# Six attention value columns and two mLSTM value columns computed by seven-product units, with a gate column moved to cover them

## The chip, the core and the metric

The kernel runs on one core of a Trainium2 chip. The metric is device time in microseconds, the median of several executions. The engines named here are TensorE (PE: matrix products and transposes), VectorE (DVE), ScalarE (ACT), GpSimd (POOL) and SyncE (SP, which here issues most of the DMA transfers).

## The reference

One step of a streaming encoder layer in fp32, for 512 prompt tokens and 64 tokens of a running stream, 576 tokens of width 1024 in all:

```
h = LN1(alpha*x + 0.5*FFN1(x))                       # SwiGLU, width 2816
z = h @ w_in      # 72 columns of 128: mLSTM q, k, v, o | gates i, f | attention q, k, v | branch gates g_m, g_a
h = LN2(alpha*h + w_out(sig(g_m)*P_m(mLSTM(h)) + sig(g_a)*P_a(BandAttn(h))))
y = LN3(alpha*h + 0.5*FFN2(h))
```

The attention has 16 heads of 64, banded over 8 chunks of 64, with a relative bias and, for the running stream, 256 cached keys and values. The mLSTM has 4 heads of 256; its output is normed within each head before its gate. The outputs are y, the mLSTM's states and the attention's k and v rows.

## The kernel before

**Columns and tokens.** Activations lie with the features on the 128 partitions and the 576 tokens along the free axis. A *column* is 128 outputs of a weight matrix. Columns of `w_in` are numbered: 0 to 7 are the mLSTM's q, 8 to 15 its k, 16 to 23 its v, 24 to 31 its o, 32 to 39 the attention's q, 40 to 47 its k, 48 to 55 its v, 56 to 63 the gates g_m, 64 to 71 the gates g_a; "if" holds the i and f gates.

**Products.** Each fp32 operand is split in a high and a low part (fp32r), and a product is three matmuls, high by high, high by low, low by high (`mm`, L133; transposes have L143). ACT makes a weight's high part (wh). The low part (wl) comes from DVE (a subtraction), or, for the columns in `ADDED`, from ACT and an accumulating DMA that POOL issues (`add_lo`). `gemm` computes columns directly: 8 blocks of k, 3 matmuls each, in two token halves (256 and 320), which is 48 matmuls a column. `Units` and its subclass `Columns` compute a pair of columns by a seven-product scheme like Strassen's: 7 products x 4 blocks x 3 matmuls of 288 tokens are 84 matmuls a pair. This needs sums of the activations (`Combos`) and sums of the pair's weights (`prep`, with parts "a", "s", "t", "u", "b"), which DVE makes and ACT and DVE split. A unit's two weight tiles are loaded by SP into wu.

**Order.** PE's instructions run in the order in which the program writes them. A planned PE time (`od.now`) advances with each matmul, and `later(dt, fn)` places a step that much later in it, so that the step's instructions stand between the matmuls then due; `drain` runs all steps that are left, whatever their due time. The other engines and DMA queues are ordered by the scheduler from that program, with priorities (`hot`, `high_priority`) and explicit "issue after" constraints. Each engine and each queue works through its own order. Weights of direct columns are loaded two ahead in the sequence `plan`, by `pump`.

**Stages around the change.**

1. The first norm (`Norm` with index 0) ends FFN1. Per token half it accumulates sums (`moments`: residual, ACT square sq, two DVE additions), places `stats` on PE `L_STATS` = 1440 ns later (sums over the features as 128x1 products with onec, rows with ones_d), then `centre`, then `spread` `L_SPREAD` = 4920 ns later, then eight `apply`s. The wave of columns 48, 40, 32 and if (`WAVE_M`, from 395.57 us) runs as the halves come free: four passes over the first token half, then the second half.
2. The mLSTM's v columns 16 and 17 follow directly (427 to 440 us); their weights are prepared early (`EARLY1`, tiles eh and el). `combos.make` makes the activation sums in the meantime.
3. Nine units (440 to about 540 us) compute the other v columns, the o columns and four gate columns; `KEEP` says what is done with each result: gates and o through a sigmoid, all stored in DRAM (VD, OD, GD) and loaded back later.
4. Eight attention heads' pairs (`att_qkv(j)` and `att_core(j)`, about 540 to 790 us). For j > 0, `att_qkv` computes directly the columns 48+j (v), 40+j (k), 32+j (q); v is turned (`v_tr`) and split into vc, k is copied and split into kh (POOL) and kl (`dup`: DVE and a cast). `att_core` computes scores, softmax, its products ptl and the values. I call each j a head below.
5. Gates, then the attention's projection, then four mLSTM heads (`ml_kq`, `ml_early`, `ml_late`; to about 1047 us). In `ml_late`, `hidden(b)` gives five result blocks, `norm` (planned at 31000 ns) norms them on DVE with a reciprocal square root on POOL (mrs), and `back(e)`, 7200 and 10600 ns behind norm, transposes them back on PE. Between the heads come no columns, and after the last one the gate columns 59 to 62:

```
    FILL = ((), (), (), (59, 60, 61, 62))
    ...
        for c in FILL[h]:
            gate(c - 56, *((sgp, "sg") if c < 60 else (None, "s")))
    del st
    od.space = 0
    od.drain()
```

6. Column 63, the mLSTM's projection with the gates, w_out, LN2 and FFN2 (1165 to 1557 us).

Of the kernel before, what the change touches and what calls it, by code (L numbers as in the profile page):

```python
# [17 lines left out]
P = 128  # L18
# [68 lines left out]
def tile_layer(ctx: ExitStack, tc: tile.TileContext, ins, outs):  # L87
# [75 lines left out]
    def blank(out, like, behind=None):  # L163
# [13 lines left out]

    ADDED = {("in", c + j) for c in (32, 40, 48) for j in range(2, KT)} | {("in", c) for c in (*range(8), *range(10, 32), *range(56, 72))} \
# [67 lines left out]
    def pump(limit=2):  # L246
        while True:
# [24 lines left out]
            if c < wst["stop"] and plan[c][0][0][:2] != "ds" and c < wst["taken"] + limit and wst["used"] < NWB:  # L272
# [3 lines left out]
                if plan[c][0] == "if":  # L276

                    r3 = raw[:, :n].rearrange("p (k c) -> p k c", c=64)
                    h3 = hi.rearrange("p (k c) -> p k c", c=P)
                    act(h3[:, :, 0:64], r3)  # L280
                    tt(h3[:, :, 64:128], r3, f(h3[:, :, 0:64]), ALU.subtract)
                    parts[c] = (hi, None)
                else:
                    lo = wpool.tile([P, 1024], F32R, tag="wl", name=nm("wl"), bufs=NWB)
                    step = n if plan[c][0] not in PIECES else 512
                    for a in range(0, n, step):

                        with tc.issue_after(k0a[0].ins) if plan[c][0] == ("in", 50) else nullcontext():
# [239 lines left out]
    class Norm:  # L528
# [98 lines left out]
        def moments(self, j, hf, dh):  # L627
# [11 lines left out]
            if j == KT - 1:  # L639
                later(L_STATS, lambda: self.stats(hf))  # L640

# [7 lines left out]
        def stats(self, hf):  # L649
# [119 lines left out]
    class Combos:  # L769
# [11 lines left out]
        def put(self, n, i, ka, kb, room, behind=None):  # L781
            t, hi, lo = self.sums[2 * i + n], room(), room()
            act(hi, t)
            if n and i < 3:
                add_lo(lo, hi, t)
            else:
                with tc.issue_after(behind.ins) if behind is not None else nullcontext():
                    tt(lo, t, f(hi), ALU.subtract)
            a, b = slice(0, HT_), slice(HT_, T)
# [100 lines left out]
    class Units:  # L890
# [3 lines left out]
        def __init__(self, srcs, j0, pool, wp, combos):  # L894
            self.srcs, self.pool, self.wp, self.x = srcs, pool, wp, combos
            self.raw, self.ws, self.p = {}, {}, {}
            self.end = len(srcs)
            self.js = list(range(j0, self.end))
# [18 lines left out]
        @hot(30)  # L917
        def lead(self, j):

            hi, lo = (wpool.tile([P, 1024], F32R, tag=t, name=nm(t), bufs=NWB) for t in ("wh", "wl"))  # L920
# [56 lines left out]
        def run(self, tail):  # L977
            cur = ahead = None
            for j in self.js + [None]:
# [13 lines left out]
                if j == self.js[0]:  # L993
                    with tc.issue_after(self.lo.ins):
                        after = self.prep(j, "u")
# [311 lines left out]
    def gate_rows():  # L1307
        yield stt(t1, fx, -1.0, fx, ALU.mult, ALU.max)
        yield act(t1, t1, AF.Exp, scale=-1.0)
# [60 lines left out]
    def att_qkv(j):  # L1370
# [15 lines left out]
        if j == 0:  # L1386
            st["G"], vp, kp = G0, vp0, kp0
            with tc.issue_after(combos.added.ins):
                for e in range(2):
# [8 lines left out]
        def v_past():  # L1398
            assert valued[0] >= 3 * (j - 1)
            for b in range(2):  # L1400
                with tc.issue_after(added["in", 50].ins) if j < 2 else nullcontext():
                    pround(vc[:, 5 + b, :, 0:64], vp4[:, b])
                tt(vc[:, 5 + b, :, 64:128], vp4[:, b], f(vc[:, 5 + b, :, 0:64]), ALU.subtract, POOL)


        later(11500 if j < 2 else 6200, v_past)
        vf = vf0 if j == 0 else slot(F32)

        def v_tr():
            assert valued[0] >= 3 * (j - 1)  # L1410
            for b0, nb in ((0, 4), (4, 1)):
# [190 lines left out]

    GD = {c: away("gd") for c in (0, 1, 2, 6, 7)}
    VD, OD = [away("vd") for _ in range(KT)], [away("od") for _ in range(KT)]
# [5 lines left out]
    def keep_o(c, tiles):  # L1610
        for e in range(2):
            act(tiles[e], tiles[e], AF.Sigmoid)
            SP.dma_start(OD[c + e], tiles[e])

    def keep_g(c, tiles):
# [3 lines left out]

    KEEP = {16: keep_v, 24: keep_o, 56: keep_g, 64: keep_g}  # L1620
    pairs = [(c, b) for c in range(0, KT, 2) for b in (16, 24)][1:] + [(0, 56), (6, 64)]
    un = Columns([(b + c, b + c + 1) for c, b in pairs],
# [19 lines left out]
    with tc.tile_pool(name="cx", bufs=1, side="right", reuse_waits="tile") as cx:  # L1642
# [3 lines left out]

        def middle():
            with tc.issue_after(q0[1].ins):
                return un.prep(0, "a")
# [29 lines left out]
    for vc in vcs:  # L1679
        for e in range(2):  # L1680
            later(11500, lambda vc=vc, e=e: blank(vc[NS:P, 4, e, :], one_[NS:P, :], added["in", 50]))
    for j in range(KT):
# [131 lines left out]
    LR = 3 + NP_ + 3 + NS  # L1814
    LU = LR - 3

    def conv_start(ct):

        R = mp.tile([P, LR], F32, tag="R", name=nm("R"))

        def cb(hf, ps):
            if hf == 0:
                POOL.memset(R[:, 0:3], 0.0)
                POOL.tensor_copy(R[:, 515:518], cols[:, C_HIST + 3 * ct:C_HIST + 3 * ct + 3])
                with tc.high_priority(offset=120):
                    act(R[:, 3:259], ps)
            else:
# [4 lines left out]
                POOL.tensor_copy(conv_st[:, ct, 3:6], R[:, 579:582])  # L1832
        return R, cb

    def conv_rest(R, ct, scale, room, tail=None):
        U = mp.tile([P, LU], F32, tag="U", name=nm("U"))
# [32 lines left out]
    def ml_kq(h):  # L1869

        st = {"k": [], "q": [], "og": [slot(F32, hp, "og") for _ in range(2)]}
        for e in range(2):
            ct = 8 + 2 * h + e
            R, cb = conv_start(ct)
            gemm(one(("in", ct)), H, [cb])
            kf, hi, lo = conv_rest(R, ct, 1.0 / 16, lambda: slot(F32R))
            st["k"].append((hi, lo))
# [8 lines left out]

            later(10600, lambda kf=kf, s=k_sink: turn5(kf, s))
        for e in range(2):
# [19 lines left out]
        for e in range(2):  # L1908
            ct = 2 * h + e
            R, cb = conv_start(ct)  # L1910
            gemm(one(("in", ct)), H, [cb])
            _, hi, lo = conv_rest(R, ct, 1.0, lambda: slot(F32R, mp, "qk", bufs=4), qtail[:, e, :])
            st["q"].append((hi, lo))
# [174 lines left out]
    for h in range(4):  # L2088
# [3 lines left out]
        for c in FILL[h]:  # L2092
            gate(c - 56, *((sgp, "sg") if c < 60 else (None, "s")))
    del st
# [21 lines left out]

    gated = [0, 1, 2, 7]
# [5 lines left out]
    for j in range(3):  # L2123
        sg[j] = slot(F32, sgp, "sg")
# [124 lines left out]
```

## Time and profile before

| | |
|---|---|
| median of 3 runs | 1560.15 us (1557.57 to 1560.44) |
| the profiled execution | 1559.5 us |
| its span | 1557.8 us |
| mean granted PE clock | 0.997 |
| PE busy | 1541.6 us (99%) |
| DVE busy | 1134.9 us (73%) |
| ACT busy | 900.1 us (58%) |

The span is the time from the first to the last instruction that the hardware profiler recorded; the execution's time holds 1.7 us more around it. Times in the lists that follow are microseconds from the span's start. A timeline row gives start, length, engine, line of the program, operation, result <- operands, tile shapes, how many instructions were grouped (x), and in brackets how long the engine had been idle before it and what ended that. A row of the chain gives start, length, engine or DMA, and tile. Matmul lengths in a timeline overlap, so the interval from one start to the next is the cost of one.

### The profile page before, as it was taken

What the parts mean: (1) busy time and instruction counts of PE and PEld (TensorE: products, weight loads), DVE (VectorE), ACT (ScalarE), POOL (GpSimd) and SP (SyncE); (2) the same over time, 40 slices, a digit from 0 to 9 for tenths busy, and PEclk for the clock granted to TensorE, in tenths of its full rate; (3) what the DMA queues carried; (4) which work ended last, traced back from release to release, by engine and by line L of the source; (5) the groups of instructions that cost most, each with busy time, mean ns of one, the idle gap of its engine ahead of it and who ended that gap; (6) DMA issues with size and microseconds to landing.
All of it is one profiled execution on the core that took longest, in us unless ns stands there. A gap on an engine that the chain in (4) does not pass through costs nothing.

```text
span 1557.8 us, 29552 instructions
## 1 busy us (share of the span) xinstructions
PE 1541.6 (99%) x11635; PEld 1525.8 (98%) x11635; DVE 1134.9 (73%) x2209; ACT 900.1 (58%) x1691; POOL 200.8 (13%) x388
## 2 busy tenths in 40 slices
PE   9999999999999999999999999999999999999998
PEld 9999999999999999999999999999999999999997
DVE  7877778656788677657677577755689887787656
ACT  7544446533766586767864877753456444457323
POOL 2000000100200043433200322202120000001000
PEclk9999999999999999999999999999999999999999
DMA  9332323534754376676534965553653323217344
GB/s 259 109 108 83 108 83 112 128 110 145 201 149 158 111 176 149 152 165 148 122 86 164 272 145 129 137 143 106 177 136 112 108 83 108 83 57 194 83 126 151
DMA packets 77876, 209.35 MB, mean 134 GB/s; under 512 B 8616, under 2 KB 20520, under 8 KB 77736
## 3 DMA queue, kind: packets, MB, share of 16 engines
q1 hardware_dynamic: 64056, 168.16, 32.7%
q0 software_dynamic: 12528, 37.59, 14.3%
q8 instruction: 91, 1.49, 0.4%
q10 hardware_dynamic: 1152, 1.70, 0.3%
q14 instruction: 49, 0.40, 0.1%
HBM read 176.95 MB, written 20.15 MB: 127 GB/s over the span
## 4 chain that ended last, share of the span: by engine, by line
PE 80%; DVE 8%; ACT 4%; DMA 4%; issue 2%; POOL 1%; SPq 0%; ACTq 0%; DVEq 0%; POOLq 0%
PE mm L133 65%; PE aux L133 13%; PE aux L143 2%; DVE wl L150 2%; DMA wr<-in_w_in 1%; ACT wh L147 1%; DMA wr<-in_w_dn 1%; DVE s L153 1%; DVE s L150 1%; ACT s L147 1%; ACT L147 0%; DVE sc L1505 0%; DMA wr<-in_w_ap 0%; DMA s<-s 0%; ACT sc L147 0%
## 5 line engine op out<-in xcount | busy, mean ns | idle before, releaser
L133 PE MATMUL mm<-s,wh 128*128 128x288 f32 (+2 forms) x3551 | 728.1, 298 | 1.1 <-DVE s L150 0.7
L133 PEld LDWEIGHTS mm<-s,wh 128*128 128x128 f32 x3551 | 570.7, 189 | 4.1 <-DVE s L150 1.6
L133 PE MATMUL mm<-s,wl 128*128 128x288 f32 (+2 forms) x1751 | 517.9, 296 | 0.0
L133 PEld LDWEIGHTS mm<-s,wl 128*128 128x128 f32 x1751 | 331.0, 189 | 0.0
L147 ACT ACTIVATE wh<-wr 128x1024 fp32r<-128x1024 f32 (+2 forms) x142 | 139.3, 983 | 148.3 <-PE mm L133 89.5
L150 DVE TENSOR_TENSOR wl<-wr,wh 128x1024 fp32r<-128x1024 f32 (+2 forms) x96 | 107.7, 1125 | 60.4 <-ACT wh L147 60.0
L133 PE MATMUL mm<-tx,wh 128*128 128x288 f32 x657 | 134.6, 296 | 0.0
L133 PEld LDWEIGHTS mm<-tx,wh 128*128 128x128 f32 x657 | 105.6, 188 | 0.0
L913 ACT ACTIVATE wh<-wt 128x1024 fp32r<-128x1024 f32 x49 | 51.9, 1060 | 85.8 <-DVE wt L150 85.8
L133 PE MATMUL mm<-tx,wl 128*128 128x288 f32 x337 | 99.3, 295 | 0.0
L150 DVE TENSOR_TENSOR wl<-wt,wh 128x1024 fp32r<-128x1024 f32 x49 | 60.0, 1225 | 50.7 <-ACT wh L913 50.6
L133 PE MATMUL mm<-h,wh 128*128 128x256 f32 (+2 forms) x384 | 78.3, 295 | 0.0
L195 POOL DMA_DIRECT2D s<-s x16 | 13.5, 845 | 491.6 <-ACT s L147 252.4
L150 DVE TENSOR_TENSOR wl<-wu,wh 128x1024 fp32r<-128x1024 f32 x47 | 57.5, 1223 | 20.6 <-ACT wh L913 20.6
L147 ACT ACTIVATE h<-h 128x288 f32<-128x288 f32 x80 | 34.9, 437 | 64.1 <-DVE h L150 64.0
L913 ACT ACTIVATE wh<-wu 128x1024 fp32r<-128x1024 f32 x47 | 49.8, 1059 | 33.5 <-PE mm L133 33.2
L133 PEld LDWEIGHTS mm<-tx,wl 128*128 128x128 f32 x337 | 63.4, 188 | 0.0
L195 POOL DMA_DIRECT2D wl<-in_w_in x44 | 38.7, 880 | 181.7 <-ACT wl L147 156.4
L133 PEld LDWEIGHTS mm<-h,wh 128*128 128x128 f32 x384 | 61.5, 188 | 0.2
L150 DVE TENSOR_TENSOR wl<-ws,wh 128x1024 fp32r<-128x1024 f32 x49 | 59.7, 1219 | 0.6 <-ACT wh L913 0.6
L150 DVE TENSOR_TENSOR ws<-wu 128x1024 f32<-128x1024 f32 x49 | 59.6, 1217 | 0.0
L913 ACT ACTIVATE ah<-wu 128x512 fp32r<-128x512 f32 x49 | 31.0, 632 | 44.6 <-PE mm L133 40.3
(396 smaller groups left out, 3671.0 us busy)
## 6 DMA issues: line engine op xcount, KB each, us to landing
wu<-in_w_gu SPq DMA_DIRECT2D x80, 512.0 KB, 4.3
wr<-in_w_in SPq DMA_DIRECT2D x54, 512.0 KB, 4.1
wl<-in_w_in POOLq DMA_DIRECT2D x44, 512.0 KB, 6.0
wr<-in_w_dn SPq DMA_DIRECT2D x40, 512.0 KB, 3.6
wu<-in_w_in SPq DMA_DIRECT2D x18, 512.0 KB, 4.9
wr<-in_w_dn SPq DMA_DIRECT2D x20, 384.0 KB, 3.5
s<-s POOLq DMA_DIRECT2D x16, 288.0 KB, 3.8
wr<-in_w_ap SPq DMA_DIRECT2D x8, 512.0 KB, 3.5
```

Of the source, the lines that this page charges most:

```text
L133: PE.matmul(out, lhsT, rhs, start=start, stop=stop, **kw)
L143: PE.transpose(out, in_, idn)
L147: return ACT.activation(out, in_, func, **kw)
L150: return (eng or DVE).tensor_tensor(out, a, b, op=op)
L153: return DVE.scalar_tensor_tensor(out=out, in0=a, scalar=s, in1=b, op0=op0, op1=op1)
L195: return POOL.dma_start(lo, src, accum_op=ALU.add)
L913: self.last = ACT.activation(hi, src, AF.Copy)
```

## The change

- Columns 16 and 17 become a unit, the first. Columns 50 to 55 (the attention's v of j = 2 to 7) become three units, the last ones. There are thirteen units for nine. `keep_a` stores the v columns in DRAM (VA) and in the output, and `att_qkv(j)` loads v from there for j >= 2; for j = 1 column 49 stays direct.
- Gate column 59 leaves the end of the mLSTM. It is computed directly behind the wave of the first norm, put through the sigmoid beside the first o unit, stored in GD[3] and loaded back with the other gates.
- No weight is prepared by `EARLY1`; instead the first unit's first weight part is made by `un.lead(0, e1)`, and the activation sums are made in another order with the rooms given by `room`. `gate_rows` is held back (12000 ns, and behind the last sum).
- In the first norm, the second token half's `stats` is placed 3200 ns behind the moments (1440 before) and its `spread` 3500 ns behind the stats (4920 before).
- `v_past` and `v_tr` are tried again 300 ns later while the values of head j - 2 haven't been issued (`once_free`).
- In the mLSTM's convolution R is one fixed tile, and the history is copied by DVE instead of POOL; one `turn5` is placed at 11800 ns instead of 10600.

```diff
-    FILL = ((), (), (), (59, 60, 61, 62))
+    FILL = ((), (), (), (60, 61, 62))
-    EARLY1 = [("in", 16), ("in", 17)]
+    EARLY1 = []
+    L_JOINT, J_SPREAD = 3200, 3500
...
-    plan_in((16, 17))
+    plan_in((59,))
     stops.append(len(plan))
     for j in range(1, KT):
-        plan_in((48 + j, 40 + j, 32 + j))
+        plan_in((*((49,) if j == 1 else ()), 40 + j, 32 + j))
...
-                later(L_STATS, lambda: self.stats(hf))
+                later(L_JOINT if hf and self.away is not None else L_STATS, lambda: self.stats(hf))
...
-            later(L_SPREAD, lambda: self.spread(hf, dg))
+            later(J_SPREAD if hf and self.away is not None else L_SPREAD, lambda: self.spread(hf, dg))
...
-        later(11500 if j < 2 else 6200, v_past)
+        later(11500 if j < 2 else 6200, lambda: once_free(v_past))
...
-        if j > 0:
-            gemm(one(("in", 48 + j)), H, [out_cb(vf, "v", j)])
-        later(2240 if j else 12500, v_tr)
+        if j == 1:
+            gemm(one(("in", 49)), H, [out_cb(vf, "v", 1)])
+        elif j:
+            SP.dma_start(vf, VA[j])
+
+        def once_free(fn):
+
+            if valued[0] < 3 * (j - 1):
+                later(300, lambda: once_free(fn))
+            else:
+                fn()
+
+        later(2240 if j else 12500, lambda: once_free(v_tr))
...
+    def keep_a(c, tiles):
+        for e in range(2):
+            SP.dma_start(VA[c + e], tiles[e])
+            SP.dma_start(outs["v"][:, c + e, :], tiles[e])
...
-    pairs = [(c, b) for c in range(0, KT, 2) for b in (16, 24)][1:] + [(0, 56), (6, 64)]
+    pairs = [(c, b) for c in range(0, KT, 2) for b in (16, 24)] + [(0, 56), (6, 64), (2, 48), (4, 48), (6, 48)]
...
-    for i, key in enumerate(EARLY1):
-        later(9000 + 4000 * i, lambda key=key: early(e1, key, EARLY1))
+    later(12500, lambda: un.lead(0, e1))
...
+    gemm(one(("in", 59)), H, [g59_cb])
...
-        combos.make(middle)
-        for c in range(2):
-            t = slot(F32, stp, "st", bufs=8)
-
-            def v_cb(hf, ps, t=t, c=c):
-                act(hs(t, hf), ps)
-                if hf == 1:
-                    SP.dma_start(VD[c], t)
-
-            gemm(one(("in", 16 + c)), H, [v_cb])
-            if c == 0:
-                with tc.issue_after(combos.last.ins):
-                    un.prep(0, "s")
-                un.prep(0, "t")
+        for i in range(4):
+            combos.put(1, i, "t2", "t4", room)
+        with tc.issue_after(combos.last.ins):
+            un.prep(0, "s")
+        un.prep(0, "t")
+        for i in range(4):
+            combos.put(0, i, "t1", "t3", room, un.lo)
+        combos.rest()
+        un.first = combos.lo
...
+        od.bg_t = od.now + 12000
         od.bg.append((GR, gate_rows()))
...
-            later(10600, lambda kf=kf, s=k_sink: turn5(kf, s))
+            later(10600 if h or not e else 11800, lambda kf=kf, s=k_sink: turn5(kf, s))
```

More of the change, by code (lines that the diff above doesn't have):

```diff
@@ L286, in pump @@
                     for a in range(0, n, step):
-                        with tc.issue_after(k0a[0].ins) if plan[c][0] == ("in", 50) else nullcontext():
+                        with tc.issue_after(k0a[0].ins) if plan[c][0] == ("in", 42) else nullcontext():
                             act(hi[:, a:a + step], raw[:, a:a + step])
@@ L896, in __init__ @@
             self.raw, self.ws, self.p = {}, {}, {}
+            self.first = None
             self.end = len(srcs)
@@ L917, in lead @@
         @hot(30)
-        def lead(self, j):
-            hi, lo = (wpool.tile([P, 1024], F32R, tag=t, name=nm(t), bufs=NWB) for t in ("wh", "wl"))
+        def lead(self, j, pool=None):
+            hi, lo = (wpool.tile([P, 1024], F32R, tag=t, name=nm(t), bufs=NWB) if pool is None else
+                      pool.tile([P, 1024], F32R, tag="l" + t, name=nm(t), bufs=1) for t in ("wh", "wl"))
             act(hi, self.raw[j][:, 0:1024])
@@ L993, in run @@
                 if j == self.js[0]:
-                    with tc.issue_after(self.lo.ins):
+                    with tc.issue_after((self.first or self.lo).ins):
                         after = self.prep(j, "u")
@@ L1307, in gate_rows @@
     def gate_rows():
-        yield stt(t1, fx, -1.0, fx, ALU.mult, ALU.max)
+        with tc.issue_after(un.first.ins):
+            yield stt(t1, fx, -1.0, fx, ALU.mult, ALU.max)
         yield act(t1, t1, AF.Exp, scale=-1.0)
@@ L1611, in keep_o @@
         for e in range(2):
-            act(tiles[e], tiles[e], AF.Sigmoid)
+            last = act(tiles[e], tiles[e], AF.Sigmoid)
             SP.dma_start(OD[c + e], tiles[e])
+        if c == 0:
+            with tc.issue_after(last.ins):
+                act(g59, g59, AF.Sigmoid)
+            SP.dma_start(GD[3], g59)
     def keep_g(c, tiles):
@@ L1815, in tile_layer @@
     LU = LR - 3
+    R = mp.tile([P, LR], F32, name="R")
+    POOL.memset(R[:, 0:3], 0.0)
     def conv_start(ct):
[L1819 removed]
         def cb(hf, ps):
             if hf == 0:
[L1823 to L1824 removed]
+                DVE.tensor_copy(R[:, 515:518], cols[:, C_HIST + 3 * ct:C_HIST + 3 * ct + 3])
                 with tc.high_priority(offset=120):
@@ L1832, in cb, with conv_rest @@
                 POOL.tensor_copy(conv_st[:, ct, 3:6], R[:, 579:582])
-        return R, cb
-    def conv_rest(R, ct, scale, room, tail=None):
+        return cb
+    def conv_rest(ct, scale, room, tail=None):
         U = mp.tile([P, LU], F32, tag="U", name=nm("U"))
@@ L2092, in tile_layer @@
         for c in FILL[h]:
-            gate(c - 56, *((sgp, "sg") if c < 60 else (None, "s")))
+            gate(c - 56, None, "s")
     del st
@@ L2122, in tile_layer @@
         SP.dma_start(m, d)
-    for j in range(3):
+    for j in range(4):
         sg[j] = slot(F32, sgp, "sg")
```

37 lines of the change are left out of this document (20 added, 17 removed).

## The prediction

> **What bounds the kernel now.** I read the page's shares and chain first, then the stages one by one in the view of stretches, then the timelines of the engines where TensorE (PE) waits.
>
> ```profile
> span 1557.8 us, 29552 instructions
> PE 1541.6 (99%) x11635; PEld 1525.8 (98%) x11635; DVE 1134.9 (73%) x2209; ACT 900.1 (58%) x1691; POOL 200.8 (13%) x388
> PE 80%; DVE 8%; ACT 4%; DMA 4%; issue 2%; POOL 1%; SPq 0%; ACTq 0%; DVEq 0%; POOLq 0%
> ...
> 484.26 38.98 PE mm L133 x291
> ...
> 780.84 28.54 PE mm L133 x213
> ```
>
> The first two lines are the span and the busy time of each engine, the third the chain by engine, the last two are steps of that chain (start, length, what, count). PE is busy 99% of the span, and the chain stays on it through long runs of matmuls. So a removed matmul is worth its issue interval, in the seven-product units (38.98 / 291 = 0.134 us) and in direct columns (28.54 / 213 = 0.134 us) alike; anything else counts only where it makes PE wait or slows its clock. Four stretches matter (columns: stretch and its length; busy us and count of PE, weight loads, DVE, ACT, POOL; granted clock; DMA share; GB/s):
>
> ```profile
> 395.57:414.52 18.95, 16.83 (x108) 15.73 (x106) 12.03 (x26) 10.61 (x21) 6.80 (x11) 0.82 0.55 166
> 401.03:407.86 6.83, 6.83 (x33) 6.83 (x34) 5.47 (x11) 2.00 (x5) 2.90 (x3) 0.50 0.54 173
> 446.00:549.00 103.00, 102.50 (x770) 101.81 (x769) 83.01 (x117) 61.25 (x97) 6.72 (x10) 1.00 0.41 134
> 643.10:672.58 29.48, 29.38 (x231) 28.70 (x230) 20.00 (x68) 21.52 (x50) 11.07 (x20) 1.00 0.64 155
> ```
>
> The first is the front of the norm behind FFN1, where PE stands still for 18.95 - 16.83 = 2.1 us; the second, inside it, ran at clock 0.50. The third is most of the nine units: PE full, DVE at 81%. The fourth is one attention head: PE full, DVE at 68%.
>
> **The change, part by part.**
>
> *Matmuls.* A pair of columns costs 2 x 48 = 96 matmuls directly and 7 x 4 x 3 = 84 as a unit. Four pairs join (16 and 17; 50 to 55 as three pairs), so 4 x 12 = 48 go: 48 x 0.134 = **-6.4 us**. That the built program has 48 PE rows fewer confirms the count. Column 59 only moves: out of the end of the mLSTM, to the place behind the norm that 16 and 17 leave. DVE gets the units' splits, at 81% of a full PE; the units hold.
>
> *The norm's front.*
>
> ```profile
> 388.72 0.80 SPq L905 DMA_DIRECT2D wu<-in_w_in  x2
> 392.44 0.33 SPq L264 DMA_DIRECT2D wr<-in_w_in  x1
> 392.44 6.07 DMA wr<-in_w_in
> 398.59 1.15 ACT L147 ACTIVATE wh<-wr 128x512 fp32r<-128x512 f32 x2 [1.69 <-DMA wr<-in_w_in]
> 398.65 0.83 PE L133 MATMUL aux<-onec,s 128*128 128x1 f32 x6 [1.13 <-DVE s L150]
> 399.64 0.45 ACT L147 ACTIVATE sq<-s 128x320 f32<-128x320 f32 x1
> 400.92 1.35 PE L133 MATMUL aux<-onec,s 128*128 128x1 f32 x6 [0.80 <-DVE s L150]
> 402.92 0.63 PE L133 MATMUL mm<-s,wh 128*128 128x256 f32 x2
> 403.56 0.63 PE L133 MATMUL mm<-s,wh 128*128 128x256 f32 x2
> 408.32 0.40 PE L133 MATMUL mm<-s,wh 128*128 128x256 f32 x2
> 408.68 0.40 PE L133 MATMUL mm<-s,wh 128*128 128x256 f32 x2
> 414.52 0.41 PE L133 MATMUL mm<-s,wh 128*128 128x320 f32 x1 [0.20 <-DVE s L150]
> ```
>
> SyncE's queue sends two loads for the units ahead of the third weight; that weight lands 6.07 us after issue, ACT waits 1.69 us for it, and the squares (399.64) stand behind in ACT's order. PE asks for the sums of the second token half at 398.65 and 400.92 and waits 1.13 and 0.80. Then its triples of matmuls step by 0.64 us (402.92 to 403.56) instead of 0.36 (408.32 to 408.68). Over 6.83 us that loses 6.83 x (1 - 0.36/0.64) = 3.0 us. With the waits at 398.65, 400.92 and 414.52 (2.1) the front holds at most 5.1 us. The change places the sums 30 matmuls after the residual is done instead of 15 (L_JOINT), the spread earlier (J_SPREAD), and the units' loads come behind the weights on the queue. I take **-4.6** for about 0.5 us of waits left; from -2.1 (waits alone) to -5.1.
>
> Here a rule of the Trainium skill is weighed, "TensorE: Matmul & The Clock Gate", section "HAM oscillation": the clock drops only after idle gaps over about 3.4 us. The trace disagrees: the half clock followed waits of 1.13 and 0.80 us. By the rule these waits would not be its cause, it would stay, and the term would be -2.1 instead of -4.6.
>
> *The start of the units.*
>
> ```profile
> 427.38 0.40 PE L133 MATMUL mm<-s,eh 128*128 128x256 f32 x2
> 428.74 1.23 DVE L150 TENSOR_TENSOR wl<-wu,wh 128x1024 fp32r<-128x1024 f32 x1 [0.84 <-ACT wh L913]
> 440.18 0.43 PE L133 MATMUL mm<-s,wh 128*128 128x288 f32 x2
> ```
>
> Between 427.38 and 440.18 PE computes columns 16 and 17, 12.8 us, while DVE and ACT make the combinations and the first unit's splits. Afterwards column 59 alone (6.4 us) covers them; for this the change makes the first split early (lead) and delays the gate rows. Following the new order by hand, the first products are met just in time: **+0.3**, from 0 to 2.5 (two splits of 1.23 uncovered).
>
> *The attention heads.* A head with v's column as a direct product gives up 48 of its matmuls, so six heads shrink from 29.48 to 29.48 - 6.43 = 23.05 us. This is in the -6.4 above, as the units pay 36 fewer than the heads save. What is left beside PE then has 6.4 us less room:
>
> ```profile
> L147 ACT ACTIVATE wh<-wr 128x1024 fp32r<-128x1024 f32 x3 | 3.2, 1057 | 0.5 <-PE mm L133 0.3
> L147 ACT ACTIVATE wl<-wh 128x1024 fp32r<-128x1024 f32 x3 | 3.2, 1052 | 0.0
> L147 ACT ACTIVATE s<-mm 128x256 f32<-128x256 f32 (+1 forms) x4 | 1.6, 401 | 0.2
> L150 DVE TENSOR_TENSOR kl<-s,kh 64x576 fp32r<-64x576 f32 x2 | 1.6, 792 | 0.6 <-POOL kh L157 0.6
> L1447 DVE CAST kl<-kl 64x576 fp32r<-64x576 f32 x2 | 1.1, 538 | 0.1
> L157 POOL TENSOR_SCALAR kh<-s 64x576 fp32r<-64x576 f32 x2 | 2.1, 1040 | 8.6 <-PE aux L133 8.5
> ```
>
> (Groups of one head: count, busy us, mean ns, idle before.) ACT loses one wh, one wl and two of the copies (2.9 us) and stands at 18.6 of 23.05 (81%). DVE loses nothing: 20.00 of 23.05, 87%. Its order matters now. In the changed order kl and its cast of a head's first half come among the scores, behind a wait for POOL's kh, and ahead of the softmax product ptl that releases the values:
>
> ```profile
> 680.29 0.69 DVE L150 TENSOR_TENSOR ptl<-aux,pth 128x512 fp32r<-128x512 f32 x1
> 682.00 0.48 PE L133 MATMUL aux<-pth,vc 128*128 128x512 f32 x1
> ```
>
> Before, ptl ends at 680.98 and is used at 682.00: 1.02 us to spare. 0.79 + 0.54 = 1.33 us put ahead of it use that up and 0.3 more; six heads, **+1.9**. Ends: 0 where the room holds, and 8.1 where DVE also stands for POOL's 1.04 us (1.35 a head). I take the small one because kh is early here: POOL idles 8.5 us of a head.
>
> The v that heads 2 to 7 load on SyncE replaces a weight load on that queue and its accumulating load on POOL's; DMA share is 0.64, so I cost it at nothing: the load hides behind the head's projections, and late it would hold only the turn of v.
>
> *The mLSTM.*
>
> ```profile
> 879.07 0.30 PE L143 MATMUL aux<-ident,qf 128*64 128x128 f32 x1 [0.83 <-DVE vl L150]
> ...
> 1038.20 0.28 PE L133 MATMUL aux<-ch,qsc 128*64 128x258 f32 x1
> ...
> 1045.59 1.25 PE L143 MATMUL aux<-ident,hf 128*128 128x128 f32 x10
> ```
>
> ```profile
> 1038.51 0.38 ACT L147 ACTIVATE hf<-aux 64x258 f32<-64x258 f32 x1 [1.57 <-PE aux L133]
> 1040.40 1.20 POOL L525 TENSOR_TENSOR mrs<-var,mhalf 128x5 f32<-128x5 f32 x1 [19.00 <-DVE var L157]
> 1041.63 0.17 DVE L150 TENSOR_TENSOR mrs<-mrs,dn 128x5 f32<-128x5 f32 x1 [1.32 <-POOL mrs L525]
> 1041.84 1.23 DVE L150 TENSOR_TENSOR wl<-wr,wh 128x1024 fp32r<-128x1024 f32 x1
> 1042.98 1.70 DVE L157 TENSOR_SCALAR hf<-hf,mv,mrs 128x256 f32<-128x256 f32 x5
> ```
>
> The turn at 879.07 is placed later (11800 for 10600) and its 0.83 us wait goes: **-0.8** (0 to -0.8).
>
> The last is the change's price. Between the last hidden product (1038.20) and the ten transposes of its normed result (1045.59) PE now has 7.4 us of matmuls, about 54; column 59 is most of them, and the built order leaves 6. Meanwhile the result's chain runs ACT, DVE, POOL, DVE, a weight split (wl, 1.23), five scalings, up to 1042.98 + 1.70 = 1044.68. It does not get shorter. Without 59 the transposes would end at 1045.59 + 1.25 - 6.43 = 1040.4; the last scaling lets them end about 1045.4. So PE loses 5.0 us. After so long a wait I expect half clock, as at 401.03; that cost 3.0, of which part falls into the wait itself: 2.4. Together **+7.4**; from 3.8 (wl slips behind the scalings, no half clock) to 8.0.
>
> *Sum:* -6.4 - 4.6 + 0.3 + 1.9 - 0.8 + 7.4 = -2.2. The profiled execution took 1559.5; 1557.3 follows, and with the median 0.65 above that execution, **1557.9 us**. A measurement of this kernel can tell about 0.2% (3.1 us) from no change: same is 1557.0 to 1563.3.
>
> **Rivals.**
>
> *A cheap end:* PE keeps its clock after the mLSTM wait (-2.4), wl slips (-1.2) and the heads are covered (-1.9): 1552.4. For it: the granted clock of the whole execution is 0.997, of which 401.03 explains 6.83 x 0.5 / 1557.8 = 0.002, so 879.07's wait cost next to no clock. Against: the wait is longer than those at the norm, which did.
>
> *DVE becomes the bound of the heads:* the wait for POOL's kh stands ahead of ptl in all six, 8.1 instead of 1.9: 1564.1, slower. It decides once a head's PE waits for DVE pass 1.35 us. For it: 87% with an order that holds it; against: POOL's idle time.
>
> *The half clock at the norm isn't made by the waits* and stays: 2.5 lost, 1560.4, no change. For it: 128x1 sums may leave PE as idle as a wait; against: triples run at full pace before the waits.
>
> *The units don't pay:* fewer matmuls, but DVE at 81% makes the four new ones wait as much as they save: 1564.3. Against: nine units in a row lose only 103.00 - 102.50 = 0.5 us.
>
> **How the numbers follow.** Forecast 0.55 (1553 to 1562), cheap end 0.12, DVE-bound heads 0.18, half clock stays 0.10, units don't pay 0.05. The range 1551.5 to 1565.0 takes in all the rivals' points and leaves out 2 in 10 for larger waits and the outer ends. Faster by over 0.2% (below 1557.0): nearly half of the forecast (0.25), the cheap end (0.12) and a little of the others: 0.40. Slower (above 1563.3): most of the DVE case, the units, and the forecast's upper tail: 0.25. Within: 0.35.
>
> **What would show it.** In the changed trace: 48 PE rows fewer; the norm's front shorter by 4 to 5 us and no clock of 0.50 there; heads of about 23.4 us with small waits on DVE; a wait of 4 to 5 us ahead of the ten transposes and triples of 0.64 us behind it. Heads of 24.5 us, or no wait at the mLSTM's end, would make the prediction wrong.

## The result and the profile after

The changed kernel took 1562.7 us (median of 11, 1561.05 to 1565.42) against 1559.5 us for the one before on the same chip: ratio 1.0029, 95% interval 1.0021 to 1.0038. (The quotient of the two medians is 1.0020, 3.2 us; the ratio 1.0029 stands for 4.5 us, and the differences between versions below go by such ratios.) It is slower by 0.2 to 0.3%. I had forecast 1557.9, 2.2 us faster and within my own bound of no change; the range held the time, the direction was wrong. The profiled execution took 1561.6 us, span 1559.8.

The page after; its first lines:

```profile
span 1559.8 us, 29470 instructions
PE 1535.2 (98%) x11587; PEld 1518.0 (97%) x11587; DVE 1169.8 (75%) x2270; ACT 894.3 (57%) x1686; POOL 182.0 (12%) x344
```

PE has 48 matmuls fewer, as counted, and is busy 6.4 us less, and yet the span is 2.0 us longer. The view of stretches shows where that went. First the kernel before, then the one after; the stretches run from the norm's wave to the second half's pass, to the last unit's end, to the attention's projection, to the first product of w_out, and to the end.

```profile
414.52:542.22 127.70, 127.20 (x943) 126.51 (x944) 103.79 (x154) 83.80 (x140) 8.22 (x11) 1.00 0.50 146
542.22:807.64 265.42, 262.98 (x2035) 255.35 (x2034) 184.38 (x585) 197.20 (x433) 88.65 (x163) 1.00 0.61 146
807.64:1103.86 296.22, 295.09 (x2254) 292.42 (x2253) 193.95 (x415) 178.63 (x370) 55.29 (x146) 1.00 0.55 151
1103.86:1557.80 453.94, 446.50 (x3370) 444.90 (x3368) 344.84 (x569) 224.58 (x380) 24.32 (x28) 1.00 0.40 119
```

```profile
394.95:408.30 13.35, 13.35 (x108) 12.76 (x106) 10.73 (x24) 7.82 (x17) 5.64 (x10) 1.00 0.81 258
408.30:574.78 166.48, 165.70 (x1232) 164.78 (x1232) 138.77 (x201) 102.78 (x170) 5.57 (x7) 1.00 0.46 146
574.78:808.43 233.65, 224.81 (x1748) 216.98 (x1746) 183.81 (x585) 178.98 (x407) 78.65 (x156) 1.00 0.56 143
808.43:1105.41 296.98, 291.80 (x2207) 287.51 (x2205) 195.65 (x431) 174.98 (x365) 50.17 (x114) 0.99 0.53 146
1105.41:1559.80 454.39, 446.59 (x3370) 444.90 (x3368) 345.06 (x569) 224.65 (x380) 24.33 (x28) 1.00 0.40 119
```

| stretch | before | after | its matmuls alone | lost |
|---|---|---|---|---|
| norm's front | 18.95 | 13.35 | 0 | -5.6 |
| second half, cover columns, units | 127.70 | 166.48 | +38.6 (288 more) | +0.2 |
| attention and gates | 265.42 | 233.65 | -38.6 (288 fewer) | +6.8 |
| projection and mLSTM | 296.22 | 296.98 | -6.4 (48 fewer) | +7.2 |
| w_out, FFN2 | 453.94 | 454.39 | 0 | +0.5 |

(Matmuls at the prediction's 0.134 us. The wave starts 0.6 us earlier, before anything that the change touches.) Hardly anything is lost at the units: they run as full as before (165.70 of 166.48 us, against 127.20 of 127.70). The attention lost 6.8 us where I had put 1.9.

PE's waits after (engine and product, what it waited for: total, times, longest), the two largest of those that are new:

```profile
PE aux L143 <- DVE mx L1510: 4.9, 3, 1.8
...
PE aux L143 <- DVE hf L157: 4.2, 1, 4.2
```

The first belongs to the attention. Two neighbouring heads after, and 14 us within the first of them:

```profile
632.92:659.77 26.85, 24.85 (x195) 23.45 (x193) 21.04 (x70) 19.28 (x48) 9.52 (x19) 1.00 0.56 145
659.77:682.46 22.69, 21.81 (x174) 21.16 (x173) 19.33 (x68) 18.14 (x44) 9.48 (x19) 1.00 0.56 137
639.67:653.67 14.00, 12.17 (x100) 11.32 (x98) 13.61 (x44) 11.11 (x28) 7.04 (x14) 1.00 0.44 126
```

Every other head is long. The six intervals without a v column, from the first scores of one head to those of the next (610.26, 632.92, 659.77, 682.46, 708.67, 731.37 and 757.51), take 22.7, 26.9, 22.7, 26.2, 22.7 and 26.1 us, 24.5 in the mean: the length that the prediction named as a sign of being wrong. DVE is busy 78% of the long one shown, but 13.61 of 14.00 us (97%) in the stretch that holds the second half of the scores. DVE's timeline there, and the PE row behind it:

```profile
648.66 0.86 DVE L150 TENSOR_TENSOR kl<-s,kh 64x576 fp32r<-64x576 f32 x1
649.55 0.16 DVE L1510 RECIPROCAL mx<-mx 128x1 f32<-128x1 f32 x1
649.74 0.67 DVE L1460 CAST kl<-kl 64x576 fp32r<-64x576 f32 x1
650.45 0.42 DVE L157 TENSOR_SCALAR sc<-sc,mx 128x384 f32<-128x384 f32 x1
...
651.01 0.52 PE L143 MATMUL aux<-ident,sc 128*128 128x128 f32 x3 [1.81 <-DVE mx L1510]
```

The next head's kl and cast stand among the softmax steps of this one, and the transposes of the scores wait 1.81 us. (The bracket names a reciprocal; the three tiles turned are those of the 384-wide scores, whose scaling ends at 650.45 + 0.42 = 650.87.)

The end of the mLSTM after, PE and then DVE:

```profile
1039.64 0.28 PE L133 MATMUL aux<-ch,qsc 128*64 128x258 f32 x1
...
1044.98 2.79 PE L143 MATMUL aux<-ident,hf 128*128 128x128 f32 x10 [4.17 <-DVE hf L157]
...
1048.21 0.63 PE L133 MATMUL mm<-s,wh 128*128 128x256 f32 x2
```

```profile
1043.28 1.23 DVE L150 TENSOR_TENSOR wl<-wr,wh 128x1024 fp32r<-128x1024 f32 x1
1044.42 1.69 DVE L157 TENSOR_SCALAR hf<-hf,mv,mrs 128x256 f32<-128x256 f32 x5
```

This went as predicted: six matmuls after the last hidden product, a wait of 4.17 us, ten transposes in 2.79 us instead of 1.25, and matmuls at half pace.

### The profile page after: what moved, and what is told of

Same layout as the page of the kernel before. It is cut to its first block, busy times and chain, and to the rows that moved or that the text cites. A ratio compares the mean times of both kernels' runs of the same rounds, so it can differ in the third digit from the quotient of the medians.

```text
span 1559.8 us, 29470 instructions
## 1 busy us (share of the span) xinstructions
PE 1535.2 (98%) x11587; PEld 1518.0 (97%) x11587; DVE 1169.8 (75%) x2270; ACT 894.3 (57%) x1686; POOL 182.0 (12%) x344
## 4 chain that ended last, share of the span: by engine, by line
PE 79%; DVE 9%; ACT 5%; issue 3%; DMA 2%; POOL 0%; SPq 0%; DVEq 0%; ACTq 0%; POOLq 0%
PE mm L133 65%; PE aux L133 12%; PE aux L143 2%; DVE wl L150 1%; DVE U L153 1%; ACT wh L147 1%; ACT sc L147 1%; DVE sc L1518 1%; DVE s L153 1%; DVE kl L150 1%; DVE s L150 1%; ACT L147 1%; DVE sc L157 0%; DMA wr<-in_w_ap 0%; DVE ptl L150 0%
## 5 line engine op out<-in xcount | busy, mean ns | idle before, releaser
L133 PE MATMUL mm<-s,wh 128*128 128x288 f32 (+2 forms) x3430 | 701.5, 298 | 0.9 <-DVE s L150 0.3
L133 PEld LDWEIGHTS mm<-s,wh 128*128 128x128 f32 x3430 | 550.0, 189 | 4.2 <-DVE s L150 0.9
L133 PE MATMUL mm<-s,wl 128*128 128x288 f32 (+2 forms) x1705 | 503.6, 295 | 0.0
L133 PEld LDWEIGHTS mm<-s,wl 128*128 128x128 f32 x1705 | 321.4, 188 | 0.5 <-DVE wl L150 0.3
L147 ACT ACTIVATE wh<-wr 128x1024 fp32r<-128x1024 f32 (+2 forms) x136 | 133.0, 979 | 144.9 <-PE mm L133 82.0
L133 PE MATMUL mm<-tx,wh 128*128 128x288 f32 x778 | 158.4, 296 | 0.0
L133 PEld LDWEIGHTS mm<-tx,wh 128*128 128x128 f32 x778 | 124.9, 188 | 0.0
L133 PE MATMUL mm<-tx,wl 128*128 128x288 f32 x383 | 113.0, 295 | 0.6 <-DVE wl L150 0.6
L133 PEld LDWEIGHTS mm<-tx,wl 128*128 128x128 f32 x383 | 72.0, 188 | 0.9 <-DVE wl L150 0.9
L133 PE MATMUL mm<-h,wl 128*128 128x256 f32 (+2 forms) x192 | 56.4, 294 | 0.0
```

Source lines behind the costliest of these rows:

```text
L133: PE.matmul(out, lhsT, rhs, start=start, stop=stop, **kw)
L147: return ACT.activation(out, in_, func, **kw)
```

## The experiments

Ratios are against runs of the kernel before on the same chip, with 95% intervals; the changed kernel has 1.0029. "Stage" is the attention from the first scores of head 0 to the attention's projection in a kernel's trace; the changed kernel's row is

```profile
582.75:808.43 225.68, 216.84 (x1687) 209.01 (x1685) 177.77 (x576) 174.06 (x399) 73.79 (x147) 1.00 0.55 137
```

**Another column as the cover.** Column 49 changes places with 59.

```diff
-    FILL = ((), (), (), (60, 61, 62))
+    FILL = ((), (), (), (59, 60, 61, 62))
-    plan_in((59,))
+    plan_in((49,))
...
-        if j == 1:
-            gemm(one(("in", 49)), H, [out_cb(vf, "v", 1)])
-        elif j:
+        if j:
             SP.dma_start(vf, VA[j])
...
```

> The changed kernel with another column as the cover behind the first norm: the attention's v column 49 (direct in head 1 so far) instead of gate column 59, which goes back to the end of the mLSTM. As many matmuls as in the changed kernel (1562.7). Theory (the wait of 4.2 us ahead of the ten transposes and the half clock behind it are there because column 59 is gone): both vanish, -7.2 us; head 1 gets shorter on PE and waits for DVE like heads 2 to 7, +1.1: about 1556.6. Rival (the norm's chain is bound by DVE, ACT and POOL whatever PE does, and the wait moves behind the transposes): 1562 to 1564.

1570.5 us, 1.0090 (1.0074 to 1.0105): both theories missed. The end did what the first said, with no wait at the ten transposes; the loss is in heads 0 and 1, which take 58.1 us (585.51 to 643.60) without column 49, against 50.2 (582.75 to 632.92) in the changed kernel. PE's timeline there, and a stretch of it at half clock; a second of 3.41 us follows the wait of 1.61:

```profile
596.94 0.44 PE L143 MATMUL aux<-ident,sc 128*128 128x128 f32 x2 [3.83 <-DVE ptl L150]
...
610.00 0.39 PE L133 MATMUL aux<-kh,qs 128*128 128x256 f32 x1 [1.61 <-DVE mx L157]
```

```profile
597.89:601.30 3.41, 3.41 (x14) 3.41 (x15) 2.59 (x13) 2.28 (x7) 0.87 (x1) 0.50 0.64 180
```

Head 0's scores run beside head 1's columns 49, 41 and 33; without 49 PE waits there. I read from it that a direct column of a head is cover for the head before it.

**The next head's low parts later.** In `dup`, kl and its cast become a step of their own.

```diff
-                tt(l_[r, cc], src[r], f(h_[r, cc]), ALU.subtract)
-                DVE.tensor_copy(l_[o, cc], f(l_[r, cc]))
+                def low():
+                    tt(l_[r, cc], src[r], f(h_[r, cc]), ALU.subtract)
+                    DVE.tensor_copy(l_[o, cc], f(l_[r, cc]))
+
+                if j:
+                    later(T_LOW + (1200 - 5240) * e, low)
+                else:
+                    low()
```

`T_LOW` is 7800 ns.

> The changed kernel with the low parts of the next head's keys (kl and its cast) placed 7800 and 9000 ns behind the k column instead of 640 and 5880. Theory (DVE's order: these four operations, 1.33 us a half, stand ahead of the softmax scaling for which the transposes wait 1.8 and 0.6 us): most of the 3.4 us of waits in a pair of heads goes, -4 of the 6.8 us that the attention lost: about 1558.7. Rival (DVE's load: it is busy without a pause for 13 us there, so that order matters little): 1 us or less, 1561.7 or above.

1.0026 (1.0016 to 1.0037). The gain of 4 us didn't come, but that tells nothing of the theories: the place in PE's planned time isn't the place in DVE's order, and kl and the cast still stood ahead of the scaling:

```profile
647.88 0.86 DVE L150 TENSOR_TENSOR kl<-s,kh 64x576 fp32r<-64x576 f32 x1
...
649.67 0.42 DVE L157 TENSOR_SCALAR sc<-sc,mx 128x384 f32<-128x384 f32 x1
```

**The norm's placing alone**, in the kernel before.

```diff
+    L_JOINT, J_SPREAD = 3200, 3500
...
-                later(L_STATS, lambda: self.stats(hf))
+                later(L_JOINT if hf and self.away is not None else L_STATS, lambda: self.stats(hf))
...
-            later(L_SPREAD, lambda: self.spread(hf, dg))
+            later(J_SPREAD if hf and self.away is not None else L_SPREAD, lambda: self.spread(hf, dg))
```

> The kernel before (1559.5) with the changed places of the second token half's sums and spread alone (3200 and 3500 ns). Theory (the placing alone removes the waits of 1.13 and 0.80 us and with them the half clock): -5 us, about 1554.5, no stretch at clock 0.50 at the norm. Rival (the third weight's late landing behind the units' loads is what delays the squares, and it is still there): a wait of about 1 us stays, the half clock with it, 1558 to 1559.5.

0.9996 (0.9987 to 1.0005). The trace is as the theory has it: the sums wait for nothing and no half clock follows. But the time hardly moves, where the theory had 5 us. That set a new question, whether the profile of before showed a common execution.

**Without the three v units**, columns 50 to 55 direct again.

```diff
-    pairs = ... + [(0, 56), (6, 64), (2, 48), (4, 48), (6, 48)]
+    pairs = ... + [(0, 56), (6, 64)]
...
+        if j:
+            gemm(one(("in", 48 + j)), H, [out_cb(vf, "v", j)])
...
```

> The changed kernel without the three units of the attention's v: columns 50 to 55 are direct in their heads again. Theory (in heads 2 to 7 PE is bound by DVE, which takes back 6.8 us of the 38.6 that leave the heads): +36 matmuls, +4.8, and -6.8 of waits: 1560.7. Rival (the attention's loss has another cause than the shorter heads): +4.8, 1567.5.

1.0013 (1.0003 to 1.0023), 2.5 us under the changed kernel with 36 matmuls more, as the theory had it (the two intervals just overlap). The stage took as long as in the kernel before (550.19 to 807.64, 257.45), and its waits for mx are gone:

```profile
550.52:807.73 257.21, 255.05 (x1975) 247.46 (x1974) 179.34 (x577) 190.50 (x423) 83.08 (x153) 1.00 0.59 145
```

So the heads' loss (6.8 us in the trace) is more than the units' gain (36 matmuls, 4.8).

**Order by constraint.** As above, but kl and cast are held behind the last scaling:

```diff
+                def low():
+                    with tc.issue_after(scaled[0].ins) if j else nullcontext():
+                        tt(l_[r, cc], src[r], f(h_[r, cc]), ALU.subtract)
+                        DVE.tensor_copy(l_[o, cc], f(l_[r, cc]))
+
+                if j:
+                    later(T_LOW + (1200 - 5240) * e, low)
...
-                ts(sc[:, :w], sc[:, :w], mx[:, 3:4], None, ALU.mult)
+                scaled[0] = ts(sc[:, :w], sc[:, :w], mx[:, 3:4], None, ALU.mult)
```

> As low_late, which left VectorE's order in the heads' busy stretch as it was; here the next head's kl and its cast are held behind the last softmax scaling of the present head by an issue constraint, so that the order does change. The changed kernel lies 4.5 us above the one before (ratio 1.0029). Order theory (kl and cast, 1.33 us a half, stand ahead of the scalings for which PE waits 1.8 and 0.6 us): about 4 of the 6.8 us come back, +0.5 against before. Load theory (DVE has its whole burst to do before the next scores, whatever the order): the waits move to the next scores, +3.5 or more.

1.0017 (1.0008 to 1.0025); stage and new waits:

```profile
583.37:807.43 224.06, 217.46 (x1687) 208.82 (x1685) 179.71 (x576) 173.42 (x399) 73.48 (x147) 1.00 0.54 139
```

```profile
PE aux L133 <- DVE o L150: 2.4, 5, 0.6
PE aux L133 <- DVE ptl L150: 1.9, 6, 0.5
```

The waits for mx are gone, and others for DVE took their place, at scores and values: 1.6 us of the 6.8 came back, less than the 4 of the order theory; the load theory's picture, waits that move, is the nearer one.

**The cast on POOL.**

```diff
-                DVE.tensor_copy(l_[o, cc], f(l_[r, cc]))
+                (pround if j else DVE.tensor_copy)(l_[o, cc], f(l_[r, cc]))
```

> The changed kernel with the cast of kl made by POOL instead of DVE in heads 1 to 7, which takes 2 x 0.54 = 1.1 us of DVE's 20 out of each head. Load theory: six heads give back about 1 us each of what they wait: -5, so -0.5 against before. Order theory: only the casts that stand in the burst count, -2, so +2.5 against before. Rival: POOL's cast is later than DVE's and the scores wait for it, no gain: +4.5 or above.

1.0022 (1.0013 to 1.0030); the stage 225.0 us, 0.7 less. Alone it gains little too, where the load theory had 5 us; the waits stay at the transposes (5.5 us in all, 6.1 in the changed kernel).

**The transposes later on PE**, behind the scaling.

```diff
-                later(2500, then)
+                later(2500 if j < 2 else 4500, then)
```

> The changed kernel with the transposes of heads 2 to 7 placed 4500 ns of planned PE time behind the scaling instead of 2500. Theory of PE's own order (the transposes stand ahead of projection matmuls that could run while DVE catches up): the waits of 1.8 and 0.6 us at the transposes go, -3.4 a pair of heads less what comes back at the values: about -5, -0.5 against before. Theory of DVE's load (a head has 20 us of DVE work in bursts that only the whole head can hold): the waits come back elsewhere, within 1 us of the changed kernel: +3.5 to +5.5.

1.0027 (1.0016 to 1.0038); two heads:

```profile
633.22:656.28 23.06, 22.72 (x182) 21.84 (x180) 20.44 (x68) 17.77 (x45) 7.56 (x14) 1.00 0.58 154
656.28:682.80 26.52, 24.91 (x195) 23.74 (x194) 20.46 (x69) 19.31 (x47) 11.66 (x25) 1.00 0.55 139
```

The long and the short head changed places; the pair takes 49.6 us, as in the changed kernel (49.5) and as the theory of DVE's load had it.

**Columns 56 and 57 as cover at the mLSTM's end**, direct instead of a unit.

```diff
-    FILL = ((), (), (), (60, 61, 62))
+    FILL = ((), (), (), (56, 57, 60, 61, 62))
-    pairs = ... + [(0, 56), (6, 64), (2, 48), (4, 48), (6, 48)]
+    pairs = ... + [(6, 64), (2, 48), (4, 48), (6, 48)]
...
```

> The changed kernel with gate columns 56 and 57 direct at the end of the mLSTM (in place of their unit), where they cover what column 59 covered; 59 stays behind the norm. 12 matmuls more: +1.6. Theory (the end's wait of 4.2 us and the half clock behind it cost 6.8 us, as the stage of v49_cover shows): -6.8, so -5.2, about -0.7 against before. Rival (the units' or the end's other waits take the place): +2 to +4.5 against before.

0.9989 (0.9980 to 0.9997), 6.2 us under the changed kernel, near the 5.2 expected. PE at the end: two groups of five transposes among matmuls, with no wait and at full clock.

```profile
1037.47 0.71 PE L143 MATMUL aux<-ident,hf 128*128 128x128 f32 x5
...
1041.10 0.71 PE L143 MATMUL aux<-ident,hf 128*128 128x128 f32 x5
```

**Without the scaling** of the softmax in heads 2 to 7, so that the output isn't the reference's.

```diff
-                ts(sc[:, :w], sc[:, :w], mx[:, 3:4], None, ALU.mult)
+                if j < 2:
+                    ts(sc[:, :w], sc[:, :w], mx[:, 3:4], None, ALU.mult)
```

> The changed kernel with the softmax scaling left out in heads 2 to 7 (the output isn't the reference's): 4.5 us of DVE work a head less, at the very place of the waits; PE's order is the same. DVE theory (in the bursts DVE is busy 97%, and PE waits for it): the attention goes back to what its matmuls need, -6.8 us, so about -2.3 against before. Rival (the chain of hops PE, DVE, ACT, DVE, PE is too long for PE's fixed order, whatever DVE's work): 2 us or less come back, +2.5 or above.

0.9988 (0.9979 to 0.9997), 6.4 us under the changed kernel; the long head and the stage:

```profile
633.22:658.05 24.83, 24.53 (x195) 23.49 (x193) 17.86 (x61) 19.27 (x48) 9.40 (x19) 1.00 0.59 158
...
583.00:803.32 220.32, 216.45 (x1686) 208.98 (x1685) 160.59 (x522) 173.87 (x399) 73.43 (x147) 1.00 0.55 140
```

5.4 of the 6.8 us come back with PE's order untouched: PE waits for DVE's work. The edit takes 17.2 us from DVE in the stage (177.77 to 160.59), 2.9 a head and not the 4.5 of the expectation. It also takes a step out of the chain from scores to transposes, so alone it doesn't tell DVE's load from the chain's length; the run with all three parts below does, as it leaves that chain whole.

**Two parts together**: the edit of `fill_5657` with that of `low_behind`, and with that of `no_v_units`.

> fill_5657 (0.9989 of before) together with low_behind (which lay 2 us under the changed kernel): if both gains add, 1557.5 - 1.7 - 2 = 1553.8, ratio 0.9975. Rival (low_behind's gain was noise): 0.9989.

> fill_5657 without the three v units: columns 50 to 55 direct in their heads. no_v_units lay 0.0016 under the changed kernel; if that adds to fill_5657, 0.9989 - 0.0016 = 0.9973 of before, 1553.3. Rival (the units' three v pairs are worth their 36 matmuls once the end is covered): 0.9989 + 0.003 = 1.002.

0.9973 (0.9963 to 0.9984), as the sum of the gains had it, and 0.9983 (0.9974 to 0.9992). The intervals overlap: with the end covered and kl behind the scaling, the three v units do no measurable harm, and no measurable good.

**All three**: the edits of `fill_5657`, `low_behind` and `cast_pool`.

> fill_behind (0.9973) with the casts of kl on POOL. Theory (DVE's work in the bursts is what PE waits for): another 1 to 2 us, 0.9963. Rival (cast_pool's gain was the same as the reordering's, not another): 0.9973.

0.9941 (0.9926 to 0.9956), 1548.8 us: much more than either theory. The long head and the stage:

```profile
620.71:646.03 25.32, 24.48 (x194) 23.45 (x193) 19.58 (x68) 19.77 (x49) 12.31 (x26) 1.00 0.50 124
...
572.54:790.50 217.96, 214.96 (x1686) 208.72 (x1685) 170.78 (x562) 173.54 (x399) 83.55 (x161) 1.00 0.55 139
```

The stage is 7.7 us shorter than in the changed kernel, where order alone gave 1.6 and the cast alone 0.7. This is the fastest version, 8.6 us under the kernel before by the medians. Against `fill_behind`, from which only the casts differ, the stage is 6.2 us shorter. That run's stage, and DVE near the end of a long head:

```profile
572.07:796.27 224.20, 217.50 (x1686) 208.80 (x1685) 179.89 (x576) 173.55 (x399) 73.76 (x147) 1.00 0.54 136
```

```profile
641.00 1.70 DVE L150 TENSOR_TENSOR kl<-s,kh 64x576 fp32r<-64x576 f32 x2
642.74 1.09 DVE L1463 CAST kl<-kl 64x576 fp32r<-64x576 f32 x2
643.86 0.69 DVE L150 TENSOR_TENSOR ptl<-aux,pth 128x512 fp32r<-128x512 f32 x1
```

With the order alone, kl and the casts stand ahead of the last ptl instead of the scaling. PE's waits for ptl and pth in the stage are 1.9 and 1.1 us there; without the casts on DVE 0.2 us for ptl is left. The softmax steps are the same in both runs, and so is v's load: neither the length of that chain nor v's load explains the loss.

**The norm at its old places** in `fill_behind`.

```diff
-    L_JOINT, J_SPREAD = 3200, 3500
+    L_JOINT, J_SPREAD = 1440, 4920
```

> fill_behind (0.9973 of before) with the sums and the spread of the first norm's second half back at their old places (1440 and 4920 ns); the loads and all else as in the changed kernel. Theory (the placing is worth the waits, 2 us, and a half clock in a part of the executions, another 1.5 on average): +3.5, ratio 0.9995. Rival (with the units' loads behind the third weight the old places do as well; front_only alone was within noise of before): 0.997 to 0.998.

0.9992 (0.9981 to 1.0004), some 3 us over `fill_behind`, near the theory's 3.5, though the two intervals just overlap. PE's wait at the sums, and the half clock behind it, 3.42 us this time:

```profile
398.41 0.83 PE L133 MATMUL aux<-onec,s 128*128 128x1 f32 x6 [0.98 <-DVE s L150]
```

```profile
400.58:404.00 3.42, 3.42 (x18) 3.42 (x18) 2.60 (x6) 1.66 (x4) 2.90 (x3) 0.50 0.88 283
```

**Both kernels profiled again**, unedited: the one before twice, the changed one once.

> The kernel before once more, for a second profiled execution. Theory (the half clock at the norm comes in a part of its executions only, as the mean clocks of 53 executions say, 0.996 to 0.999): in a trace with mean clock 0.998 or 0.999 no stretch at 0.50 lies at the norm, and the front there costs 2 us of waits, not 5. Rival (it is there each time): a stretch of 3.4 or 6.8 us at 0.50 behind 400 us again.

> The kernel before, a third profiled execution. Two showed 6.83 us at clock 0.50 at the norm; a quarter of the timed executions have a mean clock of 0.999, in which 6.8 us at half clock (0.002 of the span) beside the 5 us at the end has no room. Theory: with a mean clock of 0.998 or more, 3.4 us or nothing at half clock at the norm. With 0.997 or less: 6.8 again, which tells nothing new.

> The changed kernel, a second profiled execution. Its timed executions have mean clocks of 0.995 to 0.998, the profiled one 0.998 with 3.41 us at half clock behind the mLSTM's wait. Theory (that stretch lasts one or two windows of 3.41 us): at a mean clock of 0.996 or less it is 6.83 us there. Rival (another half clock lies elsewhere, at the attention's waits of 2 us, as in v49_cover): a stretch between 580 and 780 us.

The second execution of before took 1559.9 us at mean clock 0.996, with 6.8 us at 0.50 at the norm. The third took 1555.5 at 0.999: it has the same wait at the sums (1.12 us, as in the second; the first had 1.13 and a further 0.80) and no half clock behind it, the matmul triples stepping by 0.36 us at once.

```profile
398.05 0.83 PE L133 MATMUL aux<-onec,s 128*128 128x1 f32 x6 [1.12 <-DVE s L150]
...
400.38 0.40 PE L133 MATMUL mm<-s,wh 128*128 128x256 f32 x2
400.62 0.28 PE L133 MATMUL mm<-s,wl 128*128 128x256 f32 x1
400.74 0.40 PE L133 MATMUL mm<-s,wh 128*128 128x256 f32 x2
```

The second execution of the changed kernel took 1562.6 at 0.995, with two stretches at half clock:

```profile
651.60:655.01 3.41, 3.41 (x21) 3.37 (x19) 2.31 (x5) 0.49 (x1) 0.54 (x3) 0.50 0.82 154
1044.13:1050.96 6.83, 4.72 (x20) 4.20 (x21) 6.04 (x13) 2.21 (x4) 0.18 (x1) 0.50 0.61 196
```

Theory and rival were both right: 6.83 us at the mLSTM's end instead of 3.41, and 3.41 us more behind one of the attention's 1.8 us waits.

## Why the prediction was wrong

- **Matmuls, -6.4: right.** There are 48 fewer. That PE's busy time also falls by 6.4 us is in part chance, as half clock lengthens it: in the third execution of before it is 1538.8 us, not 1541.6.
- **Units and their start, +0.3: right** (0.2 lost in the stretch).
- **The mLSTM, -0.8 + 7.4: right in the mechanism, its closeness in part luck.** The stage lost 7.2 us, 6.6 were forecast. From the last hidden product on (1038.20 before, 1039.64 after) 6.5 us are lost, 4.4 up to the transposes and 2.2 behind them, for 5.0 and 2.4; `fill_5657` took that away. The wait of 0.83 us went, but the stretch ahead of that product grew by 0.65 us (230.56 to 231.21) instead of shrinking by 0.8; what took the gain there stays open.
- **The attention heads, +1.9: the step that failed; it measured 6.8.** I had seen that DVE would stand at 87% of a head and that kl would come into the burst of scores. But I sized it by one slack, the 1.02 us ahead of ptl, and put kl ahead of ptl; it was the scaling and the transposes behind it that were late. A slack at one row says little where the engine is busy 97% for 14 us: in `low_behind` the next steps, values and scores, were late instead. The loss was 6.8 us, near the 8.1 that I kept as the far end. The rival "DVE becomes the bound of the heads" is the case that came; its time, 1564.1, is 1.4 from the measured one. Its trigger, the wait for POOL's kh, is not what decides: DVE waited 0.3 us for kh in the two heads shown, so that the time came close is luck.
- **The norm's front, -4.6: right in the trace compared (-5.6), too large for the median.** It rested on one execution, in which 3.0 of 5.1 us were a half clock that a third execution of the same kernel doesn't have: there the front took 14.84 us (394.97 to 409.81), against 18.95 in the first and 13.35 after, so that without half clock the placing is worth 1.5. `front_only` moved the median by 0.8 us (1556.5 against 1557.4), its ratio's interval takes in 1; `fill_front_old` puts the placing at some 3 us. The value of the placing in a common execution lies between; the runs don't fix it closer. The rule that I weighed, of the Trainium skill, "TensorE: Matmul & The Clock Gate", section "HAM oscillation" (a drop only after gaps over 3.4 us), doesn't fit these traces: half clock followed waits of 0.98, 1.12, 1.81 and 1.13 + 0.80 us as well as one of 4.17. The Trainium skill says on the same page, section "What's actually happening", that the gate watches a free-running window of 3413 ns. The stretches of 3.41 and 6.83 us agree with that; that the place of a wait in such a window decides whether none, one or two of them follow is a guess, which no run here tests.
- **From the profile to the median.** I took 0.65 us of offset for both kernels. The profile of before was an execution with the half clock, that of after one with the least of it. In the traces the kernels differ by 2.0 us, in the medians by 3.2, by the ratio 1.0029 by 4.5: the change takes away a place where the clock drops in some executions and makes one where it drops in all eight traces that have the wait of 4.2 us, for 3.41 us in six of them and 6.83 in two.

Of the 4.2 us between the sum of the prediction (-2.2) and the two traces (+2.0) the heads make 4.9; the other terms nearly cancel.

What stays open: why order and cast together give so much more (7.7 us) than alone (1.6 and 0.7). The waits of the single ones fit a chain in which either delay alone is enough to keep PE waiting: with the order they move from the transposes to scores and values, with the cast they stay at the transposes. No run follows that chain step by step through a head.

## What to carry to other kernels

Matmuls that leave a stage are worth their time only as far as the other engines' bursts let PE close up: read the partner engine's busy share over the burst (14 us here), not over the stage, and expect that curing one wait can show the next. Work on the busiest engine is also cover for chains elsewhere; before moving a block, list what runs beside it at its old place (the mLSTM's norm beside 59, head 0's scores beside 49). And look at more than one execution before pricing a half clock.

## What was not expected of the hardware

The kernel before, with a wait of 1.1 us at the same row, ran on at full clock in one execution and at 0.50 for 6.8 us in two others, 1555.5 against 1559.5 and 1559.9 us. Behind a wait of 1.81 us in the attention PE ran 3.41 us at half clock in one of two executions of the changed kernel. The four versions without the waits at the norm and at the mLSTM's end (`fill_5657`, `fill_behind`, `fill_no_v`, `fill_behind_cast`) show a mean clock of 0.998 or 0.999 in all of their 36 timed executions, though `fill_5657` keeps the attention's waits of up to 1.6 us.
